# Products of two-by-two blocks in seven multiplications, in four of eleven groups of the up projection

## The chip, the cores and the metric

The kernel runs on one core of a Trainium2 chip. The time is that of the device for one launch, in microseconds, as the median of several runs. TensorE multiplies, ScalarE and VectorE prepare operands and carry results on, SyncE issues the transfers, GpSimd does almost nothing here.

## The reference

Two layers work on x, 256 tokens of width 2048, all in float32. The first part of a layer (attention and a gated spatial mix, joined by an output projection) is not touched. The second part is

```
h = rms_norm(x, norm2_g)
a = depthwise_conv_centred(h @ w_up, conv_w, conv_b)      # w_up: 2048 x 11264
g, u = split(a)                                           # 5632 columns each
x = x + (silu(g) * u) @ w_down                            # w_down: 5632 x 2048
```

The convolution runs over three neighbouring tokens, channel by channel.

## The kernel before

**Precision.** A float32 product is made of three faster ones: each operand is split into a high part and a remainder, and high x high, remainder x high and high x remainder are added in PSUM. The activations are split once per layer, the weights as they arrive: a load brings 128 x 2048 weights (1 MB) into one of four raw tiles (`rawp`), ScalarE copies out the high part (L175) and VectorE subtracts it for the remainder (L149). Both go into one of three wide places of `his` and `los`, in turn (`wide`). Waiting for them stands with TensorE, which reads them, and the next write into a place waits until TensorE has read it.

**Blocks.** One such load is a block: four row tiles of 128 by one column of 512. The tokens are two tiles of 128 (m = 0, 1), so a plain block (`direct`) is 4 x 2 x 3 = 24 matmuls of 128x512: the 16 that read the high part first, the 8 that read the remainder last.

**The up stage.** The 22 columns of 512 are taken as eleven groups j, each a gate column and an up column with 16 row tiles, so four blocks to a column. Group 0 goes through the rows with both columns side by side, since the rows are just being made; all others take the gate column whole and then the up column. Groups 0 to 4 come before the first half of the down projection, 5 to 10 before the second half. A column's sums lie in a PSUM tile of two banks; there are three such tiles (`mm`) and two of one bank (`tp`).

**What follows a column.** `leave` scales the two halves out of PSUM by each token's factor (L928) and sorts their bytes (L930); four transposing transfers on SyncE's queue (L938) turn them; two `together` copies join the bytes again (L506), each behind two transposes; then come the scales and steps of the convolution (L909, L910, L913), for the gate column SiLU (L950), for the up column the product with the gate (L958) and its split (L367, L368). `asked` and `after` let these parts in beside later blocks: the transposes one block after the column's end, the joining some blocks later.

**Order.** The engines' queues are fixed when the program is built: each engine takes its instructions in one order, and an instruction that waits holds up all behind it. What stands under `urgent()` (the splits, the leaving of a column) is placed ahead of the rest as early as the builder thinks it is ready.

**Seven products.** The down projection already uses the known scheme that multiplies 2 x 2 blocks with seven products instead of eight (`seven`, `mixed`, `seven_out`). Two row tiles by two columns by two token tiles would be eight products of three matmuls, 24; by seven they are 21. It needs sums of the activations' tiles (`mixed`, with their split, once per row pair) and sums of the weights' tiles (L261 to L263, into a second raw tile), both the load and the sums split as above (L257 and L264 on ScalarE, two L149 on VectorE), and so two wide places and two raw tiles per block. Four of the products serve more than one sum; they gather in four extra banks (`more`) over all row pairs of a column pair and are added at the end.

Of the kernel before, what the change touches and what calls it, by code (L numbers as in the profile page):

```python
# [15 lines left out]
P = 128  # L16
# [20 lines left out]
FAST = (((4, 8, 12), (4, 8, 12, 16)), ((4, 8, 12, 16), (4, 8, 12, 16)))  # L37
AFTER = (((2, 4, 5), (1, 2, 3, 4)), ((2, 4, 5, 6), (2, 4, 5, 6)))
PLACES = 6


def down_blocks(half, pair):

    f0, f1 = HALVES[half]
    c = (2 * pair, 2 * pair + 1)
    fast = FAST[half][pair]
    plain = [k for k in range(f0, f1) if k - f0 - (k - f0) % 2 not in fast]
    own = [((n,), tuple(plain[i : i + KB]), False) for i in range(0, len(plain), KB) for n in c]
    for i, k in enumerate(fast):
        own.insert(AFTER[half][pair][i] + i, (c, (f0 + k, f0 + k + 1), True))  # L50
    return own

# [8 lines left out]
def encoder(ctx: ExitStack, tc: tile.TileContext, xT, x, w_in, w_gu, w_o, w_up, w_down, wsT, pcol, prow, rope, out):  # L61
# [18 lines left out]
    def ev():  # L80
        return sl([P, 2, SEQ])
# [4 lines left out]
    def st(shape, tag):  # L86
        return small.tile(shape, F32, tag=tag, name=tag)

    def mm():
        return mmp.tile([P, 2, W], F32, tag="mm", name="mm")  # L90
# [160 lines left out]
    def seven(left, right, more, acts, mix, src, used_left, used_right, first, last):  # L251
# [33 lines left out]
        def lows():  # L285
            for ps, m, a, w, cs in low:
                nc.tensor.matmul(ps[m], a[0], w[1][:, cs], start=False, stop=ps is more and last)  # L287
            low.clear()
# [9 lines left out]
        product(left, used_left, 1, own(1, 1), (shi, slo), 3)  # L298
        lows()

    def seven_out(more, c):
# [342 lines left out]
    def next_rows(c, gain, pcs, far=False):  # L644
# [14 lines left out]
        def joined_halves():  # L659
            for j in range(2):  # L660
                t = sl([P, 2, SEQ])
                words = t.rearrange("p a b -> p (a b)").bitcast(U16).rearrange("p (n b) -> p b n", b=2)
                nc.scalar.copy(words, tall[j].rearrange("p (b a) n -> p b (a n)", b=2))
                for i in range(2):
                    g = gain + 2 * (2 * c + j) + i
                    hT.append(split_act(t[:, i, :], pcs[:, g : g + 1]))

# [29 lines left out]
    for l in range(DEPTH):  # L697
# [172 lines left out]

        hT = []
        ssq = st([P, 2, 4], "ssq")

# [43 lines left out]

        def up_rows(ps, n, j, b):
            src = w_up[l, n * (NF // 4) + j, :, b * KB * W : (b + 1) * KB * W]
            fresh = set() if b == 0 else {0, 1}  # L920
            direct([ps[:, m, :] for m in range(2)], acts2[b * KB : b * KB + KB], src, fresh, b == NB - 1)

        def leave(ps, then, wait):
            halves = []
            for m in range(2):
                rows = ev().rearrange("p a b -> p (a b)")
                with urgent():
                    nc.scalar.activation(rows, ps[:, m, :], AF.Copy, scale=r2[:, m : m + 1])  # L928
                h = sl([P, 2, 2, SEQ], U16)
                nc.scalar.copy(h, rows.bitcast(U16).rearrange("p (j n b) -> p j b n", j=2, b=2))  # L930
                halves.append(h)
# [11 lines left out]
        def gate_and_up(j, ys, mixes):  # L943
# [21 lines left out]

            if j == 0:
                pss = [mm(), mm()]
                for b in range(NB):
                    for n in range(2):
                        up_rows(pss[n], n, j, b)  # L970
                        if b == NB - 1:
                            leave(pss[n], (gate_in, up_in)[n], 2)
                return
            for n in range(2):
                ps = mm()
                for b in range(NB):
                    up_rows(ps, n, j, b)
                leave(ps, (gate_in, up_in)[n], 2 + (j == f1 // 4 - 1))

# [135 lines left out]
```

## Time and profile before

| | |
|---|---|
| three timed runs | 1953.59, 1953.72, 1954.45 us |
| the profiled execution | 1956.62 us, span 1953.7 us |
| TensorE | busy 1946.0 us of the span, 8790 matmuls in the trace |
| VectorE | busy 1404.9 us |
| ScalarE | busy 1340.8 us |
| transfers | 414 MB, mean 212 GB/s |
| granted TensorE clock | 1.000 |

A row of the chain or of a timeline is the start in us from the span's begin, a duration, and what ran (xN: so many in a row, merged); in brackets the idle time ahead of it and who ended it. A row of grouped instructions ends in busy us, mean ns of one, and idle time ahead with what ended it. A row of stages has the busy time and count of each engine. PEld is TensorE's load of its standing operand, SPq SyncE's queue of transfers. The shown duration of a matmul (0.39 us) is longer than the distance of two of them, since they overlap; the distance is what counts.

### The profile page before, as it was taken

How to read it: one execution, taken by the hardware profiler on the slowest of the kernel's cores; microseconds unless marked ns; L12 is line 12 of the kernel's file. 1: busy time of each engine (PE TensorE's matmuls, PEld its weight loads, DVE VectorE, ACT ScalarE, POOL GpSimd, SP SyncE). 2: the span in 40 equal slices, each digit the busy share in tenths (PEclk: the TensorE clock that was granted, in tenths of full speed). 3: DMA queues.
4: the chain of work that ended last, by engine and by line, in shares of the span. 5: the costliest groups of instructions: out<-in, count | busy, mean ns of one | idle time of the engine just before them, and what ended most of it. 6: DMA issues, size and time to landing. Idle time of an engine off the chain costs nothing.

```text
span 1953.7 us, 23130 instructions
## 1 busy us (share of the span) xinstructions
PE 1946.0 (100%) x8790; PEld 1614.0 (83%) x8790; DVE 1404.9 (72%) x1732; ACT 1340.8 (69%) x1473; POOL 21.3 (1%) x25
## 2 busy tenths in 40 slices
PE   9999999999999999999999999999999999999999
PEld 7888788888888888888888888888888888888887
DVE  5759775667886666779867796756669856566896
ACT  6776587777755777776776864877776557777753
POOL 0100000000000000000000000000000000000000
PEclk9999999999999999999999999999999999999999
DMA  9764586776556777656767546867775567777563
GB/s 354 219 206 151 178 256 189 220 230 212 185 219 234 205 233 225 216 173 221 236 211 236 158 153 216 235 216 221 221 215 184 221 222 217 215 209 222 173 243 131
DMA packets 191023, 414.03 MB, mean 212 GB/s; under 512 B 139456, under 2 KB 140736, under 8 KB 146112
## 3 DMA queue, kind: packets, MB, share of 16 engines
q1 hardware_dynamic: 190192, 411.83, 66.0%
q8 instruction: 68, 1.11, 0.2%
q10 hardware_dynamic: 720, 0.73, 0.1%
q14 instruction: 43, 0.35, 0.1%
HBM read 378.43 MB, written 2.10 MB: 195 GB/s over the span
## 4 chain that ended last, share of the span: by engine, by line
PE 97%; DVE 1%; ACT 0%; issue 0%; POOL 0%; DVEq 0%
PE mm L221 64%; PE mm L203 12%; PE mm L208 6%; PE mm L336 3%; PE mm L281 2%; PE mm L282 2%; PE mm L287 2%; PE mm L341 2%; PE tp L221 1%; PE tp L287 1%; PE tp L282 1%; PE tp L281 1%; PE tp L379 0%; PE tp L609 0%; PE tp L380 0%; PE tp L381 0%
## 5 line engine op out<-in xcount | busy, mean ns | idle before, releaser
L149 DVE TENSOR_TENSOR los<-raw,his 128x2048 fp32r<-128x2048 f32 (+3 forms) x476 | 867.6, 1833 | 466.3 <-ACT his L175 321.4
L221 PE MATMUL mm<-his,sl 128*128 128x512 f32 x3680 | 872.1, 389 | 0.0
L221 PEld LDWEIGHTS mm<-his,sl 128*128 128x128 f32 x3680 | 690.9, 188 | 143.2
L175 ACT ACTIVATE his<-raw 128x2048 fp32r<-128x2048 f32 (+1 forms) x236 | 446.8, 1895 | 123.0 <-PE mm L221 97.5
L221 PE MATMUL mm<-los,sl 128*128 128x512 f32 x1840 | 454.7, 389 | 0.0
L221 PEld LDWEIGHTS mm<-los,sl 128*128 128x128 f32 x1840 | 345.5, 188 | 71.6
L203 PE MATMUL mm<-his,sl 128*128 128x512 f32 x1152 | 312.2, 392 | 1.4 <-DVE sl L360 1.4
L164 ACT ACTIVATE his<-raw 128x1024 fp32r<-128x1024 f32 (+1 forms) x180 | 186.2, 1039 | 146.7 <-PE mm L203 125.5
L203 PEld LDWEIGHTS mm<-his,sl 128*128 128x128 f32 x1152 | 215.4, 188 | 47.7 <-DVE sl L360 2.9
L506 ACT COPY sl<-sl 128x1024 uint16<-128x1024 uint16 x98 | 132.3, 1350 | 119.0 <-DMA sl<-sl 119.0
L208 PE MATMUL mm<-los,sl 128*128 128x512 f32 x576 | 178.4, 390 | 1.2 <-DVE los L149 1.2
L208 PEld LDWEIGHTS mm<-los,sl 128*128 128x128 f32 x576 | 107.9, 188 | 24.4 <-DVE los L149 2.0
L264 ACT ACTIVATE his<-raw 128x2048 fp32r<-128x2048 f32 x30 | 57.4, 1914 | 63.9 <-DVE raw L263 38.6
L909 ACT ACTIVATE sl<-sl,pc 128x256 f32<-128x256 f32 x176 | 95.2, 589 | 0.9
L930 ACT COPY sl<-sl 128x1024 uint16<-128x1024 uint16 x88 | 92.0, 1046 | 2.7
L910 DVE SCALAR_TENSOR_TENSOR sl<-sl,pc 128x255 f32<-128x255 f32 x176 | 77.1, 477 | 4.5 <-ACT sl L909 4.2
L367 ACT ACTIVATE sl<-sl 128x256 fp32r<-128x256 f32 x88 | 31.9, 409 | 70.4 <-DVE sl L958 70.4
L913 DVE SCALAR_TENSOR_TENSOR sl<-sl,pc 128x255 f32<-128x255 f32 x176 | 77.0, 476 | 0.1
L257 ACT ACTIVATE his<-raw 128x1536 fp32r<-128x1536 f32 x30 | 44.6, 1487 | 28.7 <-PE mm L221 19.1
L928 ACT ACTIVATE sl<-mm,yr 128x512 f32<-128x512 f32 x88 | 59.7, 679 | 4.9 <-PE mm L221 4.9
L336 PE MATMUL mm<-sl,his 128*128 128x512 f32 x256 | 62.1, 392 | 0.0
L281 PE MATMUL mm<-his,sl 128*128 128x512 f32 x154 | 60.1, 390 | 0.0
(148 smaller groups left out, 1306.5 us busy)
## 6 DMA issues: line engine op xcount, KB each, us to landing
raw<-in_w_up SPq DMA_DIRECT2D x176, 1024.0 KB, 5.0
raw<-in_w_down SPq DMA_DIRECT2D x86, 1024.0 KB, 4.6
raw<-in_w_in SPq DMA_DIRECT2D x38, 1024.0 KB, 5.0
raw<-in_w_o SPq DMA_DIRECT2D x32, 1024.0 KB, 4.9
raw<-in_w_gu SPq DMA_DIRECT2D x16, 1024.0 KB, 5.6
sl<-sl SPq DMA_TRANSPOSE x244, 4.4
sl<-in_prow SPq DMA_DIRECT2D x12, 256.0 KB, 7.6
raw<-in_w_in SPq DMA_DIRECT2D x8, 256.0 KB, 5.8
```

The source lines that it names most:

```text
L149: nc.vector.tensor_tensor(out=lo, in0=part, in1=hi.bitcast(F32), op=ALU.subtract)
L164: nc.scalar.activation(hi[:, cs], part, AF.Copy)
L175: nc.scalar.activation(hi[:, :n], raw[:, :n], AF.Copy)
L203: nc.tensor.matmul(ps[m], acts[kk][:, part, m * P : (m + 1) * P], hi, start=first and kk == 0 and part == 0, stop=False,)
L208: nc.tensor.matmul(ps[m], acts[kk][:, 0, m * P : (m + 1) * P], lo, start=False, stop=last and kk == KB - 1)
L221: nc.tensor.matmul(ps[m], acts[kk][:, part % 2, m * P : (m + 1) * P], w, start=first, stop=done and kk == len(acts) - 1 and part == 2,)
L281: nc.tensor.matmul(ps[m], a[0], w[0][:, cs], start=new, stop=False)
L336: nc.tensor.matmul(ps[:, i, :], part_of(0, k, i), x1, start=k == 0, stop=False)
L506: nc.scalar.copy(words, tall.rearrange("p (b a) n -> p b (a n)", b=2))
L909: nc.scalar.activation(t[:, i, :], s[:, i, :], AF.Identity, bias=col(3), scale=col(1))
L910: nc.vector.scalar_tensor_tensor(out=t[:, i, 1:], in0=s[:, i, : SEQ - 1], scalar=col(0), in1=t[:, i, 1:], op0=ALU.mult, op1=ALU.add)
L930: nc.scalar.copy(h, rows.bitcast(U16).rearrange("p (j n b) -> p j b n", j=2, b=2))
```

## The change

In groups 1, 3, 6 and 8 (`UP_FAST`) the first four row tiles are taken as two row pairs (`UP_PAIRS`: rows 0, 1 and rows 2, 3), each with the gate and the up column together, by `seven`. The other twelve row tiles stay plain, three blocks to a column, and the two columns now go side by side: gate, up, **seven**, gate, **seven**, up, gate, up. When the second seven is done, `added` makes four rows of the four extra banks, and `leave` adds one to each half of the two columns before it is scaled. The activations' sums for the two row pairs are made once per layer, when the normalised rows of the second part are made (`up_mixes`). The weights of w_up are laid out on the host in the order in which they are loaded.

```
 def up_blocks(j):
+    if j not in UP_FAST:
+        rows = [tuple(range(k, k + KB)) for k in range(0, NK, KB)]
+        if j == 0:
+            return [((n,), ks, False) for ks in rows for n in range(2)]
+        return [((n,), ks, False) for n in range(2) for ks in rows]
+    plain = [k for k in range(NK) if k - k % 2 not in UP_PAIRS]
+    own = [((n,), tuple(plain[i : i + KB]), False) for i in range(0, len(plain), KB) for n in range(2)]
+    for i, k in enumerate(UP_PAIRS):
+        own.insert(UP_AFTER[i] + i, ((0, 1), (k, k + 1), True))
+    return own
...
+    def added(more):
+        t, v, r, z = row(), row(), row(), row()
+        with urgent():
+            nc.scalar.copy(t, more[0])
+            nc.vector.tensor_tensor(out=v, in0=t, in1=more[1], op=ALU.subtract)
+            nc.vector.tensor_tensor(out=r, in0=more[2], in1=v, op=ALU.subtract)
+            nc.vector.tensor_tensor(out=v, in0=v, in1=more[3], op=ALU.subtract)
+            nc.vector.tensor_tensor(out=z, in0=r, in1=more[3], op=ALU.add)
+        return [[t, v], [r, z]]
...
+                if gain == C_N2 and 2 * (2 * c + j) in UP_PAIRS:
+                    y = sl([P, 2, SEQ])
+                    for i in range(2):
+                        nc.scalar.activation(y[:, i, :], t[:, i, :], AF.Copy, scale=col(i))
+                    up_mixes.append(parts(mixed(y), [P, W]))
...
-        def leave(ps, then, wait):
+        def leave(ps, then, wait, more):
...
-                rows = ev().rearrange("p a b -> p (a b)")
                 with urgent():
-                    nc.scalar.activation(rows, ps[:, m, :], AF.Copy, scale=r2[:, m : m + 1])
+                    if more is None:
+                        rows = row()
+                        nc.scalar.activation(rows, ps[m], AF.Copy, scale=r2[:, m : m + 1])
+                    else:
+                        rows = more[m]
+                        nc.vector.tensor_tensor(out=rows, in0=ps[m], in1=rows, op=ALU.add)
+                        nc.scalar.activation(rows, rows, AF.Copy, scale=r2[:, m : m + 1])
...
+                if sevenfold:
+                    if n_fast == 0:
+                        t = mm()
+                        extra = [t[:, 0, :], t[:, 1, :], tp([P, W]), tp([P, W])]
+                    n_fast += 1
+                    seven(
+                        sums[0], sums[1], extra, acts, up_mixes[n_fast - 1], src,
+                        fresh[0], fresh[1], n_fast == 1, n_fast == len(UP_PAIRS),
+                    )
+                    if n_fast == len(UP_PAIRS):
+                        more = added(extra)
+                    continue
```

How this moves instructions, at three places. First ScalarE's queue at the end of group 0 and in group 1, layer 0. Before (L175 splits a plain block, L928 and L930 are a column's leaving, L506 joins, L909 scales, L950 is SiLU):

```order
L928 ACTIVATE sl<-mm,yr 128x512
L930 COPY sl<-sl 128x1024
L928 ACTIVATE sl<-mm,yr 128x512
L930 COPY sl<-sl 128x1024
L506 COPY sl<-sl 128x2x512
L175 ACTIVATE his<-raw 128x2048
L909 ACTIVATE sl<-sl,pc 128x256 x2
L506 COPY sl<-sl 128x2x512
L909 ACTIVATE sl<-sl,pc 128x256 x2
L506 COPY sl<-sl 128x2x512
L950 ACT_TABLE_LOAD
L950 ACTIVATE sl<-sl 128x512 x2
```

The same place now, from the join on (L534 is the join, L281 splits a seven's sums and L274 its own weights, L943 scales, L192 splits a plain block, L984 is SiLU):

```order
L534 COPY sl<-sl 128x2x512
L281 ACTIVATE his<-raw 128x2048
L943 ACTIVATE sl<-sl,pc 128x256 x2
L534 COPY sl<-sl 128x2x512
L943 ACTIVATE sl<-sl,pc 128x256 x2
L192 ACTIVATE his<-raw 128x2048
L984 ACT_TABLE_LOAD
L984 ACTIVATE sl<-sl 128x512 x2
L534 COPY sl<-sl 128x2x512
L274 ACTIVATE his<-raw 128x1536
L943 ACTIVATE sl<-sl,pc 128x256 x2
L281 ACTIVATE his<-raw 128x2048
```

Between the first seven's sums and the second's stand three joins, three pairs of scales, the SiLU and the split of the one plain block that lies between the two sevens on TensorE.

Second, VectorE's queue in the same group, now, up to the second seven's last remainder (L166 makes a remainder, L278 to L280 a seven's sums, L944 and L947 are convolution steps):

```order
L166 TENSOR_TENSOR los<-raw,his 128x1536
L278 TENSOR_TENSOR raw<-raw 128x1024
L279 TENSOR_TENSOR raw<-raw 128x512
L280 TENSOR_TENSOR raw<-raw 128x512
L166 TENSOR_TENSOR los<-raw,his 128x2048
L944 SCALAR_TENSOR_TENSOR sl<-sl,pc 128x255 x2
L947 SCALAR_TENSOR_TENSOR sl<-sl,pc 128x255 x2
```

The second seven's sums stand ahead of the first seven's last remainder, and convolution steps behind it.

Third, VectorE's queue at the end of that group, now (L992 is the product of gate and up, L396 its split, L323 to L326 make the four rows of the extra products, L961 adds them to a column's halves):

```order
L992 TENSOR_TENSOR sl<-sl 128x512
L166 TENSOR_TENSOR los<-raw,his 128x2048
L396 TENSOR_TENSOR sl<-sl 128x256 x2
L323 TENSOR_TENSOR sl<-sl,mm 128x512
L324 TENSOR_TENSOR sl<-tp,sl 128x512
L325 TENSOR_TENSOR sl<-sl,tp 128x512
L326 TENSOR_TENSOR sl<-sl,tp 128x512
L961 TENSOR_TENSOR sl<-mm,sl 128x512 x2
L166 TENSOR_TENSOR los<-raw,his 128x2048
L961 TENSOR_TENSOR sl<-mm,sl 128x512 x2
```

The reading of the extra PSUM tile (L323) stands behind the remainder of the next group's first block and behind the work of the group before.

More of the change, by code (lines that the diff above doesn't have):

```diff
@@ L38 @@
 AFTER = (((2, 4, 5), (1, 2, 3, 4)), ((2, 4, 5, 6), (2, 4, 5, 6)))
+UP_FAST = (1, 3, 6, 8)
+UP_PAIRS = (0, 2)
+UP_AFTER = (2, 3)
 PLACES = 6
@@ L50, in down_blocks, with up_blocks @@
         own.insert(AFTER[half][pair][i] + i, (c, (f0 + k, f0 + k + 1), True))
+    return own
+def up_blocks(j):
+    if j not in UP_FAST:
[7 more added lines that the diff above has]
+        own.insert(UP_AFTER[i] + i, ((0, 1), (k, k + 1), True))
     return own
@@ L871, in encoder @@
         hT = []
+        up_mixes = []
         ssq = st([P, 2, 4], "ssq")
@@ L916, in convolved @@
             return t
[L918 to L921, printed above, removed]
-        def leave(ps, then, wait):
+        def leave(ps, then, wait, more):
             halves = []
             for m in range(2):
-                rows = ev().rearrange("p a b -> p (a b)")
                 with urgent():
-                    nc.scalar.activation(rows, ps[:, m, :], AF.Copy, scale=r2[:, m : m + 1])
+                    if more is None:
[5 more added lines that the diff above has]
+                        nc.scalar.activation(rows, rows, AF.Copy, scale=r2[:, m : m + 1])
                 h = sl([P, 2, 2, SEQ], U16)
@@ L964, in up_in @@
                         waiting.append(lambda e=e, k=k: mixes.__setitem__(k, parts(e, [P, W])))
[L966 to L978, printed above, removed]
+            blocks = up_blocks(j)
+            sums, fresh, more = {}, {}, [None, None]
+            at = j * 2 * NK * W
+            n_fast = 0
+            for i, (ns, ks, sevenfold) in enumerate(blocks):
+                for n in ns:
+                    if n not in sums:
+                        t = mm()
+                        sums[n] = [t[:, m, :] for m in range(2)]
+                        fresh[n] = set()
+                src = w_up[l, :, at : at + len(ns) * len(ks) * W]
+                at += len(ns) * len(ks) * W
+                acts = [acts2[k] for k in ks]
+                if sevenfold:
+                    if n_fast == 0:
+                        t = mm()
+                        extra = [t[:, 0, :], t[:, 1, :], tp([P, W]), tp([P, W])]
[7 more added lines that the diff above has]
+                    continue
+                n = ns[0]
+                finished = not any(n in b[0] for b in blocks[i + 1 :])
+                direct(sums[n], acts, src, fresh[n], finished)
+                if finished:
+                    leave(sums[n], (gate_in, up_in)[n], 2 + (j and j == f1 // 4 - 1), more[n])
         w_at = 0
@@ L1072, in down, with up @@
         return np.ascontiguousarray(w.reshape(L, P, -1))
+    def up(w):
+        w = w.reshape(L, NK, P, 2 * NF // 4, W)
+        places = []
+        for j in range(NF // 4):
+            for ns, ks, fast in up_blocks(j):
+                if fast:
+                    places += [(ks[0], 0, j), (ks[1], 0, j), (ks[1], 1, j), (ks[0], 1, j)]
+                else:
+                    places += [(k, ns[0], j) for k in ks]
+        ks, ns, js = (np.array(v) for v in zip(*places))
+        w = w[:, ks, :, ns * (NF // 4) + js, :].transpose(1, 2, 0, 3)
+        return np.ascontiguousarray(w.reshape(L, P, -1))
     def cols(v):
@@ L1085 @@
         "w_o": blocks(a(w_o), W),
-        "w_up": blocks(a(w_up), W),
+        "w_up": up(a(w_up)),
         "w_down": down(a(w_down)),
```

4 lines of the change are left out of this document (2 added, 2 removed).

## The prediction

> **What bounds the kernel now.** I read the page's engine table and its chain first, then the chain in order of time, then the busy time by stage, then single rows where the change puts something.
>
> ```profile
> PE 1946.0 (100%) x8790; PEld 1614.0 (83%) x8790; DVE 1404.9 (72%) x1732; ACT 1340.8 (69%) x1473; POOL 21.3 (1%) x25
> PE 97%; DVE 1%; ACT 0%; issue 0%; POOL 0%; DVEq 0%
> ```
>
> TensorE is busy throughout and carries 97% of the chain, so time goes where matmuls go, as long as the other engines keep up. The chain in order of time (start, duration, what) shows how tight the matmuls lie:
>
> ```profile
> 271.83 228.48 PE mm L221 x1008
> 552.31 5.44 PE mm L221 x24
> 562.51 5.44 PE mm L221 x24
> 572.71 5.44 PE mm L221 x24
> 582.91 282.88 PE mm L221 x1248
> ```
>
> 228.48 / 1008 = 0.2267 us for a 128x512 matmul, without one gap through a whole up stage (up layer 0, first half). A plain block of 24 takes 5.44. In the down stage a plain block starts every 10.20 us where one block by seven products lies between two plain ones, so that block takes 10.20 - 5.44 = 4.76 us, which is 21 x 0.2267. The step of the change therefore already runs here at the full pace.
>
> ```profile
> core 0: us, PE busy (x) PEld busy (x) DVE busy (x) ACT busy (x) POOL busy (x), PEclk, DMA share, GB/s
> 260.00:478.00 218.00, 218.00 (x964) 180.56 (x963) 142.63 (x169) 167.00 (x175) 0.70 (x1) 1.00 0.75 224
> ```
>
> In the up stage VectorE is busy 142.63 of 218 us and ScalarE 167.00: per group of eight blocks (43.52 us) 28.5 and 33.3. That is the room the change has.
>
> **What it removes.** Each fast group loses two plain blocks (16 rows x 2 columns were 8 blocks, now 6) and gains two of seven products: 192 matmuls become 6 x 24 + 2 x 21 = 186. Four groups, two layers: 48 matmuls x 0.2267 = **10.88 us** off TensorE's path. The Trainium skill ("TensorE: Matmul & The Clock Gate", section "Back-to-back issue gap") gives about 131 ns as the sustained spacing at 512 columns; by that the sum would be an estimated 6.3 us. The 1008 matmuls above do not agree, and the measured 226.7 ns decides.
>
> **What it adds on the other engines.** Mean ns of one stand ahead of the last bar:
>
> ```profile
> L149 DVE TENSOR_TENSOR los<-raw,his 128x2048 fp32r<-128x2048 f32 x262 | 598.1, 2289 | 367.0 <-ACT his L175 321.4 <-ACT his L264 44.8 <-PE tp L282 0.4
> L175 ACT ACTIVATE his<-raw 128x2048 fp32r<-128x2048 f32 x232 | 442.6, 1909 | 119.3 <-PE mm L221 97.5 <-PE tp L221 9.6 <-PE mm L282 5.5
> L264 ACT ACTIVATE his<-raw 128x2048 fp32r<-128x2048 f32 x30 | 57.4, 1914 | 63.9 <-DVE raw L263 38.6 <-PE mm L221 22.1 <-PE mm L282 3.2
> L257 ACT ACTIVATE his<-raw 128x1536 fp32r<-128x1536 f32 x30 | 44.6, 1487 | 28.7 <-PE mm L221 19.1 <-PE mm L282 7.8 <-ACT his L175 1.6
> L149 DVE TENSOR_TENSOR los<-raw,his 128x1536 fp32r<-128x1536 f32 x30 | 52.6, 1753 | 11.9 <-PE mm L221 10.4 <-ACT his L257 1.5
> L261 DVE TENSOR_TENSOR raw<-raw 128x1024 f32<-128x1024 f32 x30 | 36.6, 1220 | 0.1
> L263 DVE TENSOR_TENSOR raw<-raw 128x512 f32<-128x512 f32 x30 | 20.6, 687 | 0.4
> L308 DVE TENSOR_TENSOR sl<-tp,sl 128x512 f32<-128x512 f32 x7 | 4.8, 683 | 0.0
> L306 ACT COPY sl<-mm 128x512 f32<-128x512 f32 x8 | 4.5, 568 | 0.8 <-PE mm L287 0.8
> ```
>
> ScalarE per fast group: two sevens 2 x (1.487 + 1.914) = 6.80, less two plain splits 3.82, plus the copy out of PSUM 0.57 = +3.55. The scaling of the four column halves stays one operation each. So 36.9 of the group's new 42.16 us (6 x 5.44 + 2 x 4.76).
> VectorE per fast group: two sevens 2 x (1.220 + 2 x 0.687 + 1.753 + 2.289) = 13.27, less 2 x 2.289 = 4.58; four subtractions and additions of what the products add, and four additions into the columns, 8 x 0.683 = 5.46; together +14.2. So 42.6 of 42.16 us: **VectorE is full in a fast group** and must catch up in the plain group behind it, where it has 43.5 - 28.5 = 15.0 us free. The additions that read PSUM and a row together do not occur in this stage before; L308 is the nearest row (683 ns), and 0.5 us either way over all of them changes nothing while they are covered.
> DMA: the weights' bytes stay (8 blocks, 8 loads of 1 MB per group), but a seven holds two of the four raw tiles.
> The four mixtures per layer (a scaled copy, three mixes, a split, twice per layer) cost ScalarE and VectorE about 3.5 us each, at the end of the output projection. There ScalarE waits for TensorE, not the reverse:
>
> ```profile
> 297.26 1.92 ACT L175 ACTIVATE his<-raw 128x2048 fp32r<-128x2048 f32 x1 [3.23 <-PE mm L221]
> ```
>
> I take 0 for them; with that cover gone it would be 3.5 us per layer.
>
> **The wait that grows.** Three wide places hold the split weights and a seven takes two. A plain block's split could so far start when the third block before it had been read; behind a seven it waits for the block just ahead of the seven, and has 4.76 us plus the last third of that block (1.81). The tightest place is the first fast group, j = 1, since j = 0 finishes both columns together, so that ScalarE does both columns' joins, scales and the SiLU just there. Before, at that place (TensorE enters j = 1 at 315.19, then ScalarE's rows and SyncE's):
>
> ```profile
> 315.19 3.79 PE L221 MATMUL mm<-his,sl 128*128 128x512 f32 x16
> 317.78 1.05 ACT L930 COPY sl<-sl 128x1024 uint16<-128x1024 uint16 x1
> 322.40 1.35 ACT L506 COPY sl<-sl 128x1024 uint16<-128x1024 uint16 x1 [3.57 <-DMA sl<-sl]
> 323.62 1.90 ACT L175 ACTIVATE his<-raw 128x2048 fp32r<-128x2048 f32 x1
> 325.43 1.08 ACT L909 ACTIVATE sl<-sl,pc 128x256 f32<-128x256 f32 x2
> 326.41 1.35 ACT L506 COPY sl<-sl 128x1024 uint16<-128x1024 uint16 x1
> 328.79 1.34 ACT L506 COPY sl<-sl 128x1024 uint16<-128x1024 uint16 x1
> 330.15 1.28 ACT L950 ACT_TABLE_LOAD   x1
> 331.45 1.15 ACT L950 ACTIVATE sl<-sl 128x512 f32<-128x512 f32 x2
> 311.80 2.50 SPq L938 DMA_TRANSPOSE sl<-sl  x2
> 314.41 0.52 SPq L173 DMA_DIRECT2D raw<-in_w_up  x1
> ```
>
> The change keeps the order up to the first join: two transposes, a load, the other transposes. I so leave that join at 322.40, behind 3.57 us in which ScalarE stands waiting for the transposes, and add starts from these rows: join 322.40, the first seven's sums 323.62 (done 325.43, wanted at 326.07 + 9 x 0.2267 = 328.11), scales, second join 326.41, scales, then the plain split behind the seven at 328.79, done 330.69 and wanted at 326.07 + 4.76 = 330.83. That just fits. Then table load and two SiLU (2.43), join 1.22, the second seven's own part 1.49: done 335.7, wanted at 336.27. Scales 0.98, its sums 1.9: done 338.6, wanted at 336.27 + 2.04 = 338.31: **0.3 us late**. VectorE then has that seven's first remainder until 337.5, four convolution steps 1.7, and the sums' remainder 2.29 from 339.1: done 341.4, wanted at 338.6 + 8 x 0.2267 = 340.4: **1.0 us late**. Together 1.3 us per layer, at the second seven of j = 1: 2.6 us in all. The bounds: 0 if the transposes land 1.3 us sooner, and 1.3 us in each of eight fast groups, 10.4, if the others are as tight.
>
> They are not by my reckoning. In j = 3, 6 and 8 the gate column left four blocks earlier, so only the up column's work falls between the sevens, without SiLU. In a steady group a join starts 7.95 us after its column starts to leave:
>
> ```profile
> 392.35 0.67 ACT L928 ACTIVATE sl<-mm,yr 128x512 f32<-128x512 f32 x1
> 400.30 1.35 ACT L506 COPY sl<-sl 128x1024 uint16<-128x1024 uint16 x1 [2.19 <-DMA sl<-sl]
> ```
>
> By the same adding of rows from j = 1 on, ScalarE comes to that leave 2.5 us into j = 3, since the fast group before left both its columns late; the join follows at 10.5, scales, the split behind the seven 12.7 to 14.6, wanted at 15.64. Slack 1.0, and 2 us at the second seven. I take 0 there.
>
> **Sum:** 10.88 - 2.6 = 8.3 us saved. The profiled span is 1953.7 and its run took 1956.62; the three timed runs have a median of 1953.72, about the span. Taken from the median: **1945.4 us**. A measurement of this kernel tells about 0.2%, 3.9 us, from no change.
>
> **The rivals.**
> *Everything is hidden* (17%): the transposes land sooner, no block waits: 1953.72 - 10.88 = 1942.8. For it: the down stage runs seven, plain, seven without a gap. Against it: there ScalarE has no joins to wait for.
> *Every fast group pays about what j = 1 pays* (22%): 8 x 1.3 = 10.4 us, so 1953.2; with half of it 1948. For it: VectorE's 42.6 of 42.16 us and only 1.0 us of slack at j = 3. Against it: the plain group behind each fast one has 15 us to recover.
> *VectorE falls behind and holds the PSUM tile* (8%): slower. The four extra products use the third of three two-bank tiles; the next group's first column gets it only when VectorE has made the first subtraction, which in its queue stands behind four plain splits and a column's convolution. Adding its rows from 341.4 on (4 x 2.29 splits, six steps and two products about 5, waits for ScalarE about 0.5) it comes at about 356.2, and TensorE wants the tile at 315.19 + 42.16 + 1.3 = 358.65: slack 2.4. A longer wait for transposes ahead of it eats that:
>
> ```profile
> 358.28 1.36 ACT L506 COPY sl<-sl 128x1024 uint16<-128x1024 uint16 x1 [5.50 <-DMA sl<-sl]
> ```
>
> If VectorE comes 5.5 us later, each of eight groups waits 3.1: 24.8 - 8.3 = 16.5 us slower, 1970. It is slower at all from 2.4 + 8.3 / 8 = 3.4 us on. The skill's page on TensorE (section "Why this matters for your kernels") warns that idle gaps over about 3 us bring the clock to half; by that each such gap would cost more. No run here shows it: the granted clock is 1.00 in the stage above.
> *The change doesn't do what it says* (3%): the 21 matmuls take as long as 24 because of what lies between them: no change, 1953.7. The 10.20 us above speak against it.
>
> **How the numbers follow.** Forecast 50% (own range 1943.5 to 1949), hidden 17%, every group pays 22%, slower 8%, no effect 3%. Range 1942 to 1952: it leaves out the slower case and the top of "every group pays". Faster by over 0.2% holds for the forecast, "hidden" and the mildest quarter of "every group pays": 0.72. Within 0.2% the rest of that one and "no effect": 0.20. Slower: 0.08.
>
> **What would show it.** TensorE has 48 fewer matmuls at the same 0.2267 us. Its only new waits: about 1.3 us in each layer at the second seven of j = 1, released by ScalarE's or VectorE's seven split. Waits at the split behind a seven in j = 3, 6 or 8 would mean "every group pays"; waits at the start of j = 2, 4, 7, 9 released by VectorE's subtraction the PSUM tile; no wait at all "hidden". VectorE's busy time should rise by about 8 x 14.2 + 7 = 121 us, ScalarE's by 8 x 3.55 + 7 = 35. The forecast is wrong if the up stage's blocks no longer lie end to end outside j = 1.

## The result, and the profile after

The changed kernel takes 1943.45 us (median of 4 runs, 1942.77 to 1944.57), the kernel before 1954.01 us beside it: 10.56 us less, a ratio of 0.9945 with an interval of 0.9933 to 0.9958. A second measurement (e_again below) gave 0.9950 (0.9938 to 0.9963). The forecast was 1945.4 us, with a range of 1942 to 1952; the rival "everything is hidden" stood at 1942.8, so the time alone does not tell the two apart.

The profiled execution after, from the page (its run took 1943.45 us):

```profile
span 1941.6 us, 23236 instructions
PE 1934.0 (100%) x8742; PEld 1604.8 (83%) x8742; DVE 1517.0 (78%) x1876; ACT 1372.1 (71%) x1509; POOL 22.9 (1%) x25
PE 96%; DVE 2%; ACT 1%; DMA 1%; issue 0%; SPq 0%; POOL 0%; DVEq 0%; ACTq 0%
```

TensorE has 48 matmuls less (8790 to 8742) and still bounds everything. VectorE is busy 112.1 us more than before (1404.9), ScalarE 31.3 us more (1340.8).

Where the 10.6 us are is read from the chain of waits in order of time (start, duration, what). After:

```profile
269.75 43.19 PE mm L238 x191
340.15 70.73 PE mm L238 x312
579.18 65.28 PE mm L238 x288
864.10 10.88 PE mm L238 x48
1234.83 43.55 PE mm L238 x192
1304.72 70.75 PE mm L238 x312
1543.76 65.28 PE mm L238 x288
1828.68 10.88 PE mm L238 x48
```

The same places before, as far as the prediction has not shown them:

```profile
870.55 10.88 PE mm L221 x48
1242.07 228.48 PE mm L221 x1008
1553.16 282.88 PE mm L221 x1248
1840.81 10.88 PE mm L221 x48
```

The starts cut each layer into two pieces: from the start of the up projection to the last two plain blocks of the first half's down projection, and from there to the two plain blocks behind the first seven of the second half's down projection. Each piece holds two fast groups, which take 2 x 6 x 0.2267 = 2.72 us off TensorE if nothing waits. The rows give:

| piece | before | after | less | of it matmuls | waits |
|---|---|---|---|---|---|
| layer 0, first half | 311.08 | 309.43 | 1.65 | 2.72 | 1.07 |
| layer 0, second half | 287.64 | 284.92 | 2.72 | 2.72 | 0 |
| layer 1, first half | 311.09 | 308.93 | 2.16 | 2.72 | 0.56 |
| layer 1, second half | 287.65 | 284.92 | 2.73 | 2.72 | 0 |

So 10.88 us of matmuls left, and 1.6 us of waits came, both in first halves. From there to the next layer's up projection (864.10 to 1234.83, before 870.55 to 1242.07) another 0.8 us went. Of the waits that the profile counts for TensorE's matmuls after, only those of the first row lie in an up projection (total, times, longest); the second row is the same two, counted for its weight loads:

```profile
PE mm L304 <- DVE los L166: 0.9, 2, 0.7
PEld mm L304 <- DVE los L166: 1.7, 2, 1.1
```

L304 is the group of matmuls with remainders inside a block by seven products; the two waits are the second seven of j = 1, once per layer. There, in layer 0, TensorE, ScalarE and VectorE did this (start, duration, what, idle time before):

```profile
338.96 0.50 PE L304 MATMUL mm<-los,sl 128*128 128x512 f32 x1 [0.67 <-DVE los L166]
...
356.32 3.79 PE L238 MATMUL mm<-his,sl 128*128 128x512 f32 x16
```

```profile
326.37 1.90 ACT L192 ACTIVATE his<-raw 128x2048 fp32r<-128x2048 f32 x1
328.30 1.28 ACT L984 ACT_TABLE_LOAD   x1
...
331.85 1.48 ACT L274 ACTIVATE his<-raw 128x1536 fp32r<-128x1536 f32 x1
333.23 1.08 ACT L943 ACTIVATE sl<-sl,pc 128x256 f32<-128x256 f32 x2
334.22 1.91 ACT L281 ACTIVATE his<-raw 128x2048 fp32r<-128x2048 f32 x1
```

```profile
335.83 0.87 DVE L947 SCALAR_TENSOR_TENSOR sl<-sl,pc 128x255 f32<-128x255 f32 x2
336.62 2.28 DVE L166 TENSOR_TENSOR los<-raw,his 128x2048 fp32r<-128x2048 f32 x1
...
352.79 0.68 DVE L323 TENSOR_TENSOR sl<-sl,mm 128x512 f32<-128x512 f32 x1
```

ScalarE's split of the sums (L281) ends at 336.13. VectorE is then in the convolution until 336.6, and its remainder of the sums (L166) ends at 338.90; TensorE starts on it at 338.96. The last row is the first subtraction of the join: it lets go of the third PSUM tile at 353.47, and TensorE goes on with j = 2 at 356.32, without a wait. The tile had 2.85 us to spare. (A bracket counts from the shown end of the matmul before, which is later than the distance of starts: the 0.67 us are 0.83 from start to start, and 1.05 with the matmuls beside it, which is the 1.07 of the table.)

### The profile page after: what moved, and what is told of

Its sections match the earlier page's. It is cut to its first block, busy times and chain, and to the rows that moved or that the text cites. A ratio compares the mean times of both kernels' runs of the same rounds, so it can differ in the third digit from the quotient of the medians.

```text
span 1941.6 us, 23236 instructions
## 1 busy us (share of the span) xinstructions
PE 1934.0 (100%) x8742; PEld 1604.8 (83%) x8742; DVE 1517.0 (78%) x1876; ACT 1372.1 (71%) x1509; POOL 22.9 (1%) x25
## 4 chain that ended last, share of the span: by engine, by line
PE 96%; DVE 2%; ACT 1%; DMA 1%; issue 0%; SPq 0%; POOL 0%; DVEq 0%; ACTq 0%
PE mm L238 58%; PE mm L220 13%; PE mm L225 7%; PE mm L364 3%; PE mm L304 3%; PE mm L298 3%; PE mm L299 2%; PE mm L369 2%; PE tp L238 1%; PE tp L304 1%; PE tp L298 1%; PE tp L299 1%; DVE los L166 1%; DMA sl<-sl 1%; PE tp L407 0%; PE tp L637 0%
## 5 line engine op out<-in xcount | busy, mean ns | idle before, releaser
L166 DVE TENSOR_TENSOR los<-raw,his 128x2048 fp32r<-128x2048 f32 (+3 forms) x492 | 895.3, 1830 | 305.3 <-ACT his L192 152.7
L238 PE MATMUL mm<-his,sl 128*128 128x512 f32 x3424 | 811.6, 389 | 0.0
L238 PEld LDWEIGHTS mm<-his,sl 128*128 128x128 f32 x3424 | 642.8, 188 | 133.4
L192 ACT ACTIVATE his<-raw 128x2048 fp32r<-128x2048 f32 (+1 forms) x220 | 415.8, 1894 | 127.8 <-PE mm L238 92.7
L238 PE MATMUL mm<-los,sl 128*128 128x512 f32 x1712 | 423.1, 389 | 0.0
L238 PEld LDWEIGHTS mm<-los,sl 128*128 128x128 f32 x1712 | 321.4, 188 | 66.7
L220 PE MATMUL mm<-his,sl 128*128 128x512 f32 x1152 | 310.7, 391 | 0.4 <-ACT his L181 0.4
L220 PEld LDWEIGHTS mm<-his,sl 128*128 128x128 f32 x1152 | 215.4, 188 | 45.2 <-ACT his L181 0.8
L225 PE MATMUL mm<-los,sl 128*128 128x512 f32 x576 | 178.1, 390 | 1.3 <-DVE los L166 1.3
L534 ACT COPY sl<-sl 128x1024 uint16<-128x1024 uint16 x98 | 132.4, 1351 | 56.2 <-DMA sl<-sl 55.7
L281 ACT ACTIVATE his<-raw 128x2048 fp32r<-128x2048 f32 x46 | 88.0, 1913 | 64.3 <-DVE raw L280 38.6
L225 PEld LDWEIGHTS mm<-los,sl 128*128 128x128 f32 x576 | 108.0, 188 | 23.9 <-DVE los L166 1.7
L943 ACT ACTIVATE sl<-sl,pc 128x256 f32<-128x256 f32 x176 | 95.5, 590 | 1.3
L298 PE MATMUL mm<-his,sl 128*128 128x512 f32 x234 | 91.3, 390 | 0.0
L299 PE MATMUL mm<-his,sl 128*128 128x512 f32 x234 | 91.0, 389 | 0.0
L274 ACT ACTIVATE his<-raw 128x1536 fp32r<-128x1536 f32 x46 | 68.3, 1484 | 28.6 <-PE mm L238 19.1
L944 DVE SCALAR_TENSOR_TENSOR sl<-sl,pc 128x255 f32<-128x255 f32 x176 | 79.2, 479 | 8.3 <-ACT sl L943 7.5
L947 DVE SCALAR_TENSOR_TENSOR sl<-sl,pc 128x255 f32<-128x255 f32 x176 | 78.1, 478 | 0.6
L304 PE MATMUL mm<-los,sl 128*128 128x512 f32 x234 | 75.7, 390 | 0.9 <-DVE los L166 0.9
```

The costliest lines, as they stand in the source:

```text
L166: nc.vector.tensor_tensor(out=lo, in0=part, in1=hi.bitcast(F32), op=ALU.subtract)
L192: nc.scalar.activation(hi[:, :n], raw[:, :n], AF.Copy)
L220: nc.tensor.matmul(ps[m], acts[kk][:, part, m * P : (m + 1) * P], hi, start=first and kk == 0 and part == 0, stop=False,)
L225: nc.tensor.matmul(ps[m], acts[kk][:, 0, m * P : (m + 1) * P], lo, start=False, stop=last and kk == KB - 1)
L238: nc.tensor.matmul(ps[m], acts[kk][:, part % 2, m * P : (m + 1) * P], w, start=first, stop=done and kk == len(acts) - 1 and part == 2,)
L298: nc.tensor.matmul(ps[m], a[0], w[0][:, cs], start=new, stop=False)
```

## The experiments

In the table, "waits" is what the four pieces above take beyond their matmuls (starts in each kernel's own chain; 0.2267 us a matmul), idle time and slower matmuls alike, in the order layer 0 first and second half, layer 1 first and second half. "Sum" is before's 1954.0 less the matmuls saved plus all waits, to be held against the median.

| kernel | fast groups | waits, us | sum | median | ratio to before (interval) |
|---|---|---|---|---|---|
| after | 1, 3, 6, 8 | 1.07, 0, 0.56, 0 | 1944.7 | 1943.45 | 0.9945 (0.9933 to 0.9958) |
| e_again | 1, 3, 6, 8 | 1.38, 0, 0.68, 0 | 1945.2 | 1944.17 | 0.9950 (0.9938 to 0.9963) |
| e_mixes_only | none | 0, 0, 0, 0 | 1954.0 | 1953.77 | 0.9998 (0.9990 to 1.0007) |
| e_no_silu0 | 1, 3, 6, 8 | 1.86, 0, 0.67, 0 | 1945.7 | 1944.78 | 0.9950 (0.9938 to 0.9963) |
| e_apart | 1, 3, 6, 8 | 0.35, 0, 2.10, 0 | 1945.6 | 1945.38 | 0.9955 (0.9943 to 0.9968) |
| e_early | 1, 3, 6, 8 | 2.00, 0.10, 1.94, 0 | 1947.2 | 1946.32 | 0.9964 (0.9951 to 0.9976) |
| e_later | 2, 4, 6, 8 | 6.95, 0, 4.88, 0 | 1954.9 | 1953.25 | 0.9997 (0.9989 to 1.0006) |
| e_j4_plain | 2, 6, 8 | 0.36, 0, 0, 0 | 1946.2 | 1946.98 | 0.9962 (0.9950 to 0.9975) |
| e_five | 1, 3, 5, 7, 9 | 1.08, 1.99, 1.02, 1.69 | 1946.2 | 1946.46 | 0.9964 (0.9950 to 0.9977) |
| e_eight | 1 to 4, 6 to 9 | 11.30, 5.77, 10.75, 4.27 | 1964.3 | 1964.54 | 1.0048 (1.0034 to 1.0062) |
| e_eight_unjoined | 1 to 4, 6 to 9 | 3.92, 0, 2.24, 0.14 | 1938.5 | 1941.27 | 0.9935 (0.9921 to 0.9948) |
| e_held | 1, 3, 6, 8 | 10.41, 10.66, 8.82, 10.52 | 1983.5 | 1983.64 | 1.0152 (1.0138 to 1.0165) |

The sums meet the medians within 1.7 us, e_eight_unjoined within 2.8; so the pieces account for the times. The intervals of the kernels at 0.9945 to 0.9964 overlap, so what sets these apart is read from the traces. One caution for all of them: the order of each engine's queue is planned from the program, and every edit here, however small, has it planned anew from the edited place on (in e_no_silu0 ScalarE's queue is the changed kernel's up to the SiLU, and differs in many places behind it). None of these kernels differs in one instruction alone, so each is read from its own trace.

**The mixtures alone.** `UP_FAST = ()`; the mixtures of the activations are still made.

```
-UP_FAST = (1, 3, 6, 8)
+UP_FAST = ()
```

> All eleven groups are plain again; what stays of the change is only the four mixtures per layer at the end of the output projection (their copies, mixes and splits, read by nobody). My theory (they lie behind ScalarE's waits for TensorE and cost 0): as before, 1954.0 us, within 1 us, and an up stage of 228.48 and 282.88 us without a wait. Rival (the mixtures are on the path, about 3.5 us in each layer): up to 1961, with TensorE waiting at the end of the output projection or at the start of the up projection; then the sevens saved more than 10.88 and the 10.6 us of the change is a net of the two.

Measured: 1953.77 us. The up stages are again without a gap, and the first starts no later than before (its row of the chain):

```profile
270.71 228.48 PE mm L238 x1008
```

The mixtures cost nothing that can be measured, so the gain comes with the sevens.

**The changed kernel again.** No edit.

> The changed kernel itself, beside the three others on one chip. Both theories: 1943.5 us, waits of about 1.05 and 0.56 us at the second seven of j = 1 and no others in the up projection. If the waits differ by more than 0.3 us in the same order of instructions, what the profile shows of single waits is no better known than that.

Measured: 1944.17 us, the same two waits and no others in the up projection; the first-half pieces waited 1.38 and 0.68 us instead of 1.07 and 0.56. So a wait in one profile is known to about 0.3 us.

**The SiLU of j = 0 left out.**

```
-                    nc.scalar.activation(y, y, AF.Silu)
+                    if j:
+                        nc.scalar.activation(y, y, AF.Silu)
```

> As the changed kernel, but the SiLU of group j = 0 is left out (the gate columns of that one group go on unrounded by it, so the output is not the reference's); its table load goes with it. That takes 1.28 + 1.15 us from ScalarE just ahead of the second seven of j = 1 and nothing from VectorE. My theory (ScalarE, which does both joins, the scales and the SiLU of j = 0 there, brings the second seven's split late, and VectorE's remainder of the sums follows it): the wait of 1.05 us (layer 0) and 0.56 us (layer 1) at the second seven of j = 1 is gone, 1.6 us less than the changed kernel, 1941.8 us. Rival (VectorE alone is late there, with its convolution and the remainders of both sevens, or the weights of that seven land late): the wait stays at 0.5 to 1 us, about 1943.4.

Measured: 1944.78 us, 2.5 us of waits; neither theory's number. The wait at the second seven is gone in both layers, but two others of nearly the same size came in layer 0, both released by ScalarE's split of a plain block right behind a seven, in j = 1 and in j = 3:

```profile
341.51 3.92 PE L238 MATMUL mm<-his,sl 128*128 128x512 f32 x16 [0.71 <-ACT his L192]
417.83 3.92 PE L238 MATMUL mm<-his,sl 128*128 128x512 f32 x16 [0.55 <-ACT his L192]
```

ScalarE's 2.4 us do lie on the way to the second seven. Taking them away did not shorten the half, because the new order is late at other blocks: in the changed kernel the split for the block behind the second seven followed the seven's own at once (336.03 us); here a join and its scales stand between them.

**The sevens further apart.** Later second seven (e_apart), earlier first seven (e_early):

```
-UP_AFTER = (2, 3)
+UP_AFTER = (2, 4)      e_apart
+UP_AFTER = (1, 3)      e_early
```

> The second block by seven products of a fast group comes one plain block later (two plain blocks between the two sevens instead of one); number of matmuls as in the changed kernel. My theory (the wait is at the second seven of j = 1 and only because ScalarE's and VectorE's queues are 1 us late there): the wait of 1.05 and 0.56 us vanishes, 1941.8 us. Rival (what the products add is then joined later and VectorE holds the PSUM tile: the first subtraction was done 2.85 us before TensorE wanted the tile, and now starts up to 5.44 us later): TensorE waits up to 2.6 us at the start of each group behind a fast one, 8 x 2.6 = 21 us, total up to 1963, by waits that VectorE's subtraction releases.

> The first seven of each fast group one plain block earlier (one plain block ahead of it, two between the sevens), the second seven and the join behind it where they were. My theory (the wait at the second seven of j = 1 is ScalarE's work that queues up between the two sevens; the first seven's splits now lie where ScalarE stood waiting for the transposes): no wait at the second seven of j = 1, 1.6 us less than the changed kernel, 1941.8 us. Rival (each fast group's order is a new one and some other block is late by about as much, as with the SiLU left out): 0.5 to 2.5 us of waits per first half at other blocks, 1943 to 1946 us.

Measured: 1945.38 and 1946.32 us. Both times the wait at the second seven of j = 1 was gone, and j = 3 waited instead at its first seven, in e_apart in layer 1, in e_early in both layers:

```profile
1376.62 0.50 PE L298 MATMUL mm<-his,sl 128*128 128x512 f32 x1 [1.75 <-ACT sl L958]
```

```profile
406.71 0.50 PE L298 MATMUL mm<-his,sl 128*128 128x512 f32 x1 [1.62 <-ACT sl L958]
```

```profile
402.00 1.90 ACT L281 ACTIVATE his<-raw 128x2048 fp32r<-128x2048 f32 x1
...
405.97 0.68 ACT L958 ACTIVATE sl<-mm,yr 128x512 f32<-128x512 f32 x1
```

The first row is e_apart in layer 1, the others e_early in layer 0. The extra products of a seven need the third PSUM tile, which held the up column of the group before; ScalarE copies that column out (L958) behind a join, its scales, the seven's split and half a SiLU, and ends at 406.65. This is a holder of the tile that the prediction did not name: ScalarE on the way in, not VectorE on the way out. So e_early's rival, another block late by as much, came true, and neither run reached the 1941.8 us of my theory.

**Other places for the fast groups.** Shifted by one in the first half (e_later), and the same without j = 4 (e_j4_plain):

```
-UP_FAST = (1, 3, 6, 8)
+UP_FAST = (2, 4, 6, 8)      e_later
+UP_FAST = (2, 6, 8)         e_j4_plain
```

> The fast groups are j = 2, 4, 6, 8 instead of 1, 3, 6, 8, the number of matmuls is the same. My theory (the wait of 1.05 and 0.56 us in j = 1 comes from the work of j = 0's two columns that finish together, and no fast group that follows a plain one with staggered columns waits): no wait of TensorE in any fast group, 1.6 us less than the changed kernel, 1941.8. Rival A (the first fast group of a half pays, wherever it lies, since the pipeline of joins is disturbed by it): the same 1.6 us shows up in j = 2, total 1943.5. Rival B (VectorE full, the group before the down projection cannot be repaid there): no wait in j = 2, but waits at the first blocks of the down projection behind j = 4, 1 to 3 us per layer, total 1943 to 1948.

> Fast groups j = 2, 6, 8 alone: against the kernel with j = 2, 4, 6, 8 (1953.25 us, 11.8 us of waits in the two first halves) only j = 4 is plain again, 12 matmuls more. My theory (the waits came from the fast group that lies right ahead of the down projection: no plain group repays VectorE there, and the down projection starts with sevens of its own): 36 matmuls per two layers less than before, 8.2 us, and at most the 0.8 us wait in j = 2 of one layer: 1954.0 - 8.2 + 0.8 = 1946.6 us. Rival (a fast j = 2 was what upset the order of the queues, and j = 4 only inherited its delay): waits of 4 us and more per first half stay, total 1954 or more.

Measured: e_later 1953.25 us, the whole gain gone; e_j4_plain 1946.98 us, as expected. My theory of the wait (j = 0's two columns) failed in e_later, and its rival B, waits in the down projection behind j = 4, was right for the larger part: counted from the starts of TensorE's matmuls, 4.0 and 3.3 us of the two first halves' waits lie there, where it had 1 to 3. It had not the 1.7 and 1.6 us within j = 4 and the 1.2 us in layer 0's j = 2. The longest waits of TensorE in layer 0:

```profile
372.14 0.50 PE L304 MATMUL mm<-los,sl 128*128 128x512 f32 x1 [0.81 <-DVE los L166]
...
460.55 3.92 PE L238 MATMUL mm<-his,sl 128*128 128x512 f32 x16 [1.38 <-ACT his L192]
508.24 2.11 PE L238 MATMUL mm<-los,sl 128*128 128x512 f32 x8 [1.15 <-DVE los L166]
...
549.41 0.50 PE L298 MATMUL mm<-his,sl 128*128 128x512 f32 x1 [0.46 <-DVE xr L721]
```

The first row is the first seven of j = 2, the second the plain block behind the first seven of j = 4, the last two already the down projection, where some 60 us after the end of the up projection a seven still waits for VectorE (L721 adds the residual). With j = 4 plain the first halves wait 0.36 and 0 us, j = 2 included. So in these two orders a fast group is cheap where a plain group lies behind it, and j = 4, with the down projection's own sevens behind it, costs 5 to 7 us. That VectorE and ScalarE catch up in the plain group is the likely reason, not shown apart.

**A fifth group.** `UP_FAST = (1, 3, 5, 7, 9)`.

> Five fast groups, j = 1, 3, 5, 7, 9, each with a plain group behind it: 12 matmuls less than the changed kernel, 2.72 us. My theory (a fast group costs no wait where the group behind it is plain and lies in the same half, since VectorE's subtraction then comes 9 us and more ahead of the end of its group as in j = 3, 6 and 8): 1943.45 - 2.7 = 1940.7 us, TensorE's only waits in the up projection those of j = 1. Rival (j = 5 comes straight behind the down projection of the first half, whose sevens have loaded VectorE and ScalarE, so it pays as j = 1 does or more): 1 to 3 us of waits per layer in j = 5, total 1942 to 1946.

Measured: 1946.46 us, not the 1940.7 of my theory: the rival's size, not its place. The second halves wait 1.99 and 1.69 us, more than the 1.36 us that their third fast group saves, and layer 1's up stage starts with a wait of 1.6 us:

```profile
690.47 0.50 PE L304 MATMUL mm<-los,sl 128*128 128x512 f32 x1 [0.42 <-DVE los L166]
778.32 3.93 PE L238 MATMUL mm<-his,sl 128*128 128x512 f32 x16 [0.85 <-ACT his L192]
1236.68 3.96 PE L238 MATMUL mm<-his,sl 128*128 128x512 f32 x16 [1.60 <-ACT his L192]
```

The first two are the first seven of j = 7 and the plain block behind the first seven of j = 9. The third wait, 1.60 us, also stands in e_eight and e_eight_unjoined, so it does not come from the fifth group alone.

**Eight groups,** with no plain group between them, with and without the join, and with GpSimd making the sums:

```
-UP_FAST = (1, 3, 6, 8)
+UP_FAST = (1, 2, 3, 4, 6, 7, 8, 9)            e_eight
-                        more = added(extra)
+                        pass                  e_eight_unjoined, too
-            nc.vector.tensor_tensor(out=s[...  e_eight_pool, too (three lines)
+            nc.gpsimd.tensor_tensor(out=s[...
```

> Eight fast groups, j = 1, 2, 3, 4 and 6, 7, 8, 9, so that no plain group lies between them: another 48 matmuls less, 10.88 us. My theory (VectorE has about 28.5 + 13.1 = 41.6 of the 42.16 us of a fast group, and the PSUM tile came free 2.85 us before TensorE wanted it): VectorE just keeps pace, the one wait left is that of j = 1, total 1943.45 - 10.9 = 1932.6. Rival (VectorE falls behind without a plain group to recover in, since it also stands idle some 2.5 us per group behind ScalarE's splits and the transposes): each fast group behind another then goes at VectorE's pace, about 44.6 us, and TensorE waits 2.4 us in each of 12 groups less what the first slack takes: 25 us lost against 10.9 gained, total about 1955, with waits released by VectorE at the splits or at the start of the groups.

> The eight adjacent fast groups again, with the join left out: what the four extra products hold is never read or added (so the output is not the reference's). That takes one copy from ScalarE and eight operations of 0.68 us, 5.5 us per fast group, from VectorE, and lets the PSUM tile go at once. My theory (VectorE's load and the tile it holds made the adjacent groups wait): of the 32 us of waits most go, 1933 to 1942 us. Rival (ScalarE's splits, the joins of the transposes and the two raw tiles of a seven set the pace of adjacent fast groups): only the 11 us of waits for the tile go, 1950 to 1955 us.

> The eight adjacent fast groups once more (1964.5 us, 32 us of waits), with the three additions that make the sums of each seven done by GpSimd, in the down projection too. That takes 2.6 us per seven from VectorE, 5.2 of about 41.6 us in a fast group. My theory (VectorE's load is what made the adjacent groups wait: its subtraction held the PSUM tile, 11.1 us in 6 waits, and its remainders came late): most waits go, 1936 to 1948 us, with GpSimd busy some 60 x 4 us. Rival (the sums come later by GpSimd, and with them the split, the remainder and the release of the two raw tiles that a seven holds, so that the weights' loads are late): waits remain, now released by ScalarE's splits and the loads, 1955 to 1975 us.

Measured: 1964.54, 1941.27 and 2036.07 us (the last a ratio of 1.0416, 1.0402 to 1.0430). In e_eight, 96 fewer matmuls than before (21.8 us) are paid with 32 us, most of them waits, some 6 us slower matmuls behind four of the waits (the last section has them). The largest rows:

```profile
PE mm L238 <- DVE sl L323: 11.1, 6, 2.4
PE mm L304 <- DVE los L166: 3.3, 7, 0.7
```

The largest is the PSUM tile held by VectorE's subtraction, the prediction's slower rival; this run's rival (25 us of waits) was right in kind and somewhat too small, my "just keeps pace" was wrong. Leaving the join out took 5.5 us per fast group from VectorE and freed the tile, and 26 of the 32 us went; what stayed is a remainder or a split some 0.4 to 0.7 us late, as in j = 1. So it is the join that closes the way to more groups; its time and the tile were taken away together, so this run does not part them. Moving the sums to GpSimd made it far worse, by both sides: GpSimd takes 2.6 to 3.1 times VectorE's time for the same additions (3128 against 1220 ns, 2143 against 686), and VectorE's own operations on two SBUF operands grew beside it. In e_eight, then e_eight_pool:

```profile
L992 DVE TENSOR_TENSOR sl<-sl 128x512 f32<-128x512 f32 x44 | 30.2, 686 | 0.4
L278 DVE TENSOR_TENSOR raw<-raw 128x1024 f32<-128x1024 f32 x62 | 75.7, 1220 | 37.1 <-DMA raw<-in_w_up 28.5 <-DMA raw<-in_w_down 8.4
```

```profile
L992 DVE TENSOR_TENSOR sl<-sl 128x512 f32<-128x512 f32 x44 | 43.0, 977 | 0.8
L278 POOL TENSOR_TENSOR raw<-raw 128x1024 f32<-128x1024 f32 x62 | 193.9, 3128 | 961.8 <-DMA raw<-in_w_up 337.1 <-DMA raw<-in_w_down 261.0 <-DVE los L166 142.8
```

An operation that reads PSUM (L961) kept its time, 678 ns against 680. The Trainium skill ("SBUF — State Buffer", section "SBUF: two separate sides") says that VectorE, with two operands in SBUF, and GpSimd lock each other out of a shared pair of ports for a whole instruction; these rows agree in direction, 42% longer with two operands in SBUF and no longer with one in PSUM. The rival of this run had the right sign, not the right place: the largest waits were VectorE's subtraction again:

```profile
PE mm L238 <- DVE sl L323: 45.4, 12, 7.0
```

**The tile held longer.** VectorE repeats its first subtraction:

```
+            for _ in range(9):
-            nc.vector.tensor_tensor(out=v, in0=t, in1=more[1], op=ALU.subtract)
+                nc.vector.tensor_tensor(out=v, in0=t, in1=more[1], op=ALU.subtract)
```

> VectorE repeats its first subtraction eight times (the same result, 8 x 0.61 = 4.9 us more of its time) in every fast group, ahead of the release of the third PSUM tile. In the changed kernel that tile came free 2.85 us before the end of j = 1 and 9.2 to 11.6 us before the ends of j = 3, 6 and 8. My theory (the PSUM tile decides only beyond that slack): waits released by the subtraction only at the start of j = 2, of 2.0 us per layer if just the repeats delay it, up to 6.4 if the two remainders that now stand between the repeats do too, none at the starts of j = 4, 7 and 9: 1947.5 to 1956 us. Rival (VectorE's total load is what counts, 41.6 + 4.9 of 42.16 us in every fast group): waits in all eight fast groups or those behind them, 8 x 4 = 32 us, about 1975.

Measured: 1983.64 us, outside both theories' times and nearer to the rival's 1975 than to my 1947.5 to 1956. Four waits, not two and not eight (the repeated subtraction is L324 in this kernel): at the start of j = 2 in each layer 7.04 and 6.84 us, near the 6.4 that the slack of 2.85 us gave, and at the start of j = 9, 7.5 and 7.7 us, which I did not expect. There the new order had put the join later: it began 39 us into j = 8, in the changed kernel 32. None at the starts of j = 4 and j = 7. So with the same load added to all eight groups only those wait whose subtraction came too late for the tile; the load alone does not decide, but why the order put j = 8's join later stays open. The four waits make 29.1 us, but the run is 39.5 us longer than e_again. Some 9 of the other 10 us are TensorE's clock. The first 16 matmuls behind the wait, then the stretches around it (the window, its length, busy times of the engines, and last but two the granted clock):

```profile
362.86 5.94 PE L238 MATMUL mm<-his,sl 128*128 128x512 f32 x16 [7.04 <-DVE sl L324]
```

```profile
355.40:362.80 7.40, 0.43 (x2) 0.00 (x1) 7.23 (x9) 0.62 (x1) 0.00 (x0) 0.84 0.56 170
362.80:366.00 3.20, 3.14 (x8) 2.49 (x9) 3.20 (x6) 1.90 (x3) 0.00 (x0) 0.50 0.73 289
369.00:372.00 3.00, 3.00 (x15) 2.49 (x14) 1.21 (x1) 3.00 (x3) 0.00 (x0) 1.00 0.46 90
```

These 16 take 5.94 us where 16 take 3.79 elsewhere: this wait of 7 us costs 9, and the four cost 8.4 to 10.3 each.

## Why the prediction was right, point by point

- **The time:** 1943.45 us lies nearer to "hidden" (1942.8) than to the forecast. What decides for the forecast is that the two waits it named came, at their place, and no others in the up projection; that the time fell 1.9 us below it is 1.0 us of smaller waits and a gain elsewhere that nobody forecast (the last point).
- **What bounds it, and the 10.88 us:** right. Without the sevens the time is that of before (0.9998); with them, the second halves shorten by 2.72 us each, to the hundredth.
- **The mixtures at 0:** right, by e_mixes_only. The row at 297.26 us with which I backed it does not show it: it lies 25 us inside the up projection, and the mixtures are made ahead of that.
- **The wait at the second seven of j = 1:** right in place and in who releases it, too large in size: 1.07 and 0.56 us, not 1.3 twice. In layer 0 the term that was mis-sized is the 0.3 us of ScalarE. The join came 6.88 us into the group, not 7.21 (two joins lie between the two sevens' sums, as the sum had it, not three), so the split of the sums ended at 336.13, while TensorE reached that part at 336.22. In e_again, the same order, the 0.3 us were there (337.69 us), and layer 0 waited 1.38. VectorE's 1.0 us stood in layer 0, and about half of it in layer 1, which is the larger miss. That it is ScalarE's and VectorE's queues between the two sevens is supported by e_no_silu0, e_apart and e_early, in each of which this wait went. That j = 0's two columns are its cause is likely but not shown: no second seven behind a plain group with staggered columns waits in the changed kernel or in e_later, but e_later waited 0.81 us at the first seven of layer 0's j = 2, where VectorE had stood idle for that seven's weights:

```profile
367.20 1.23 DVE L278 TENSOR_TENSOR raw<-raw 128x1024 f32<-128x1024 f32 x1 [3.33 <-DMA raw<-in_w_up]
```

- **No wait in j = 3, 6 and 8:** right in the changed kernel, but the slack of 1.0 us at the plain block behind a seven was no safe margin. In e_no_silu0 that block of j = 3 is 0.55 us late, in e_five that of j = 9 is 0.85 us late.
- **"Every fast group pays":** did not happen in this kernel. With the groups elsewhere (e_five) five of the ten fast groups wait, by 0.5 to 1.5 us from start to start.
- **"VectorE holds the PSUM tile":** did not happen in this kernel; the slack was 2.85 us, I had 2.4. The mechanism is real: it is the largest wait in e_eight and the only large one in e_held. "VectorE is full in a fast group" was not: it is busy 33.8 of 43.2 us in layer 0's j = 1 and 36.8 of 42.1 in j = 3, since part of a group's work is done in the next one. The fullest stretch is ScalarE's in the plain group behind, 41.7 of 43.5 us in j = 2. The price per microsecond was too low, since it left the clock out.
- **The added load:** VectorE 112 us instead of 121, ScalarE 31 instead of 35. I added single durations; neighbouring operations overlap by about 0.08 us (two of L961 take 1.28, one 0.68), which over VectorE's 144 added instructions would be some 11 us, an estimate; 9 are missing.
- **The rest:** 10.88 less 1.63 is 9.25, and 10.56 was measured. 0.8 us of the difference lies between the pieces of the two layers (370.73 us instead of 371.52), in a stretch to which the change adds only layer 1's mixtures. It arises 121 to 124 us into it, where before one of layer 1's first matmuls waits 0.24 us for VectorE (L360) and those beside it lose the rest, and after none does. e_again, e_apart and e_early have it too (370.7 to 370.8), e_mixes_only not (371.52), so it goes with the new order and is luck for the forecast; what in the order does this stays open. The 0.5 us that are left lie inside the interval. The spans of the two profiles differ by 2.1 us more, ahead of the up projection (269.75 against 271.83); after and e_again, of the same order, differ there by 1.2, so medians are compared and not spans.

## What to carry to other kernels

Where TensorE is full, taking matmuls away pays at their full rate only as long as what feeds it arrives in time: here four groups of eleven with a plain group behind each gave 0.5%, five gave no more, eight lost, and four with two of them shifted by one place gave nothing. Price such a change by its release points (which buffer, whose queue, how long before it is wanted) rather than by busy totals, and take the slack of a planned order as good for that order alone. No arrangement that was tried beats the changed kernel, except one that leaves the join out and so computes something else.

## What the runs showed of the hardware

TensorE's granted clock fell after waits that the prediction's estimate took as plain idle time. In e_eight the waits of 2.39 and of 2.02 us, and two like them in layer 1, were each followed by 16 matmuls in about 5.5 us instead of 3.8. In e_eight_pool one of 1.92 us was, too, and one of 2.35 us was not:

```profile
445.17 5.54 PE L238 MATMUL mm<-his,sl 128*128 128x512 f32 x16 [2.39 <-DVE sl L323]
769.17 5.53 PE L238 MATMUL mm<-his,sl 128*128 128x512 f32 x16 [2.02 <-DVE sl L323]
```

```profile
446.00:449.00 3.00, 3.00 (x9) 2.33 (x8) 3.00 (x5) 0.95 (x2) 0.00 (x0) 0.57 0.45 188
```

```profile
744.19 5.53 PE L238 MATMUL mm<-his,sl 128*128 128x512 f32 x16 [1.92 <-DVE sl L323]
...
453.65 3.92 PE L238 MATMUL mm<-his,sl 128*128 128x512 f32 x16 [2.35 <-DVE sl L323]
```

The third row is the stretch behind the first: granted clock 0.57, and 0.50 from 446.40 to 449.81. In all traces kept here, no wait up to 1.77 us showed such a loss, and each of 3.7 us and more did. Between the two it went both ways: 1.78 us lost in e_eight_pool (at 1935.58 us), 3.48 us did not (at 1419.57 us). So the length of a wait in that range does not decide; what else does was not tested. The Trainium skill ("TensorE: Matmul & The Clock Gate", section "Why this matters for your kernels") warns of gaps over about 3 us; here 1.78 us was once enough, and 3.48 us once was not. A loss makes a wait dearer by some 1.7 us, in e_held by up to 2.8, and it is why holding the tile was worse than its idle time.
